# AdaLN projections past the first 2048 columns: row tiles summed by VectorE, partitions by TensorE

## The chip, the core and the metric

The kernel runs on one core of a Trainium2 chip. The metric is the device time of one execution in microseconds, taken as the median of several runs. TensorE (PE) multiplies matrices, VectorE (DVE) and ScalarE (ACT) do elementwise work, GpSimd (POOL) a few masks, and SyncE (SP) issues most of the DMA transfers.

## What is computed

The reference is a two-layer diffusion backbone on 256 latent and 256 context tokens with 1024 channels. Cut to what matters here:

```python
for i in range(DEPTH):                                    # DEPTH = 2
    mod_x = split(silu(c)     @ w_ada[i] + b_ada[i], 6)   # w_ada[i] is (1024, 6144)
    mod_c = split(silu(c_ctx) @ w_ada[i] + b_ada[i], 6)
    hx = rmsnorm(xs, norm1_g) * (1 + mod_x[1]) + mod_x[0] # the same for cs with mod_c
    mx, mc = token_mixers(hx, hc)    # w_in, four mixers, gated branch products, w_out
    xs = xs + mod_x[2] * mx
    xs = xs + mod_x[5] * swiglu(modulate(rmsnorm(xs, norm2_g), mod_x[3], mod_x[4]))
    # the context stream cs likewise with mod_c, except in the last layer
return rmsnorm(xs, final_norm_g)
```

Each `mod` is a product of one vector (one for the latent stream, one for the context) with a matrix of 1024 rows and 6144 columns: 24 MB of weights per layer for very little arithmetic.

## The kernel before

All activations lie with channels on partitions, as tiles of 128 channels by up to 512 tokens (256 latent, then 256 context). The large weights come as one stream `wst` of chunks of eight 128 x 128 blocks. `w_load` issues a chunk's load of 512 KB on SP into one of six buffers named `raw`; `w_ensure` cuts a chunk into two parts, `whi` (a copy by ScalarE) and `wlo` (two subtractions of 128 x 512 by VectorE), two chunks ahead of their use. Every block then takes three matmuls (`mm3`) into one of four banks `mm`, by way of `linear`. The mixers and small sums use four other banks `mx`.

A layer runs in three stages. In the mixers' stage, `interleave` traces the generator `lin` (products of `w_in`, later the gates and the branch products) beside the mixers' generators, by model clocks, so that TensorE and VectorE both have work. Then `out_by_stream` multiplies by `w_out` and normalizes, and SwiGLU follows: in layer 0 two groups of 11 column tiles, each tile the two products `pa` and `pg` and the function `swi`, and after each group the product with `w_ffn_out`. Layer 0 handles 512 tokens through its end, layer 1 mostly 256. A scheduler of the framework then orders each engine's instructions by modelled readiness and priority. Matmuls of the mixers and of adaLN stay behind the products traced before them (`who["now"]`).

The first 2048 columns of adaLN of layer 0 are made at the start (`ada_now`) and the last 1024 of layer 1 in its `w_out` stage. The rest are generators in the list `fill`: `ada_steps(l, c0, w)` makes 4 `w` columns. Each call of `filler` goes one step on in the first generator of the list. A step loads the columns of one row tile (128 of the 1024 rows) into one or two `raw` buffers; the next step multiplies them on TensorE, four matmuls side by side that each fill 32 rows of the bank:

```python
for j in range(4):
    PE.matmul(ps[32 * j:32 * j + 32, 0:w], cs[:, k, :], ..., start=k == 0, stop=k == KD - 1, tile_position=(0, 32 * j))
```

`cs` holds the two conditioning vectors in columns 0 and 1 of 32, the rest zero; the sum over the eight row tiles is accumulated in the bank. At the end `ada_finish` copies the bank (ScalarE), transposes blocks of 128 columns (TensorE) and adds the bias into `mods` (VectorE). `filler` is called after most products of `lin`, in `out_by_stream`, in `swi` and after the tiles of `w_ffn_out`; with these calls all generators of both layers are done by 620 us, inside the mixers' stage of layer 0.

Of the kernel before, what the change touches and what calls it, by code (L numbers as in the profile page):

```python
# [19 lines left out]
KD = D // 128  # L20
# [10 lines left out]
# on-chip room: slots, buffers of weights (raw, cut), chunks loaded and cut ahead of their use, banks for products  # L31
# [4 lines left out]
# per layer: the mixers (ssm, mla, ret) whose products are in float32 rather than in three of float32r  # L36
FP = ("m", "sr")
# per layer: the mixers that run one after the other, and those beside them (c: conv)
MIX = ("smr c", "smr c")
# per layer: lead of the products over the mixers, what a mixer's vector time counts for, gates computed ahead  # L40
# [4 lines left out]
# columns of w_in  # L45
# [7 lines left out]
# per-channel parameters, one column per tile of 128 channels  # L53
# [22 lines left out]
def n_blocks():  # L76
    """Blocks of [128, 128] of the weights of all layers, with room for the places left free to align some."""
    return L * (70 * KD + 18 + 16 + 128 + 64 + 3 * KD * KF + 32) + (L - 1) * (64 + 11 * KD)
# [13 lines left out]
class Slots:  # L92
    """Tiles of up to 2 KiB per partition, and halves of such; a tile is given back in program order."""
# [28 lines left out]
    def pair(self, n):  # L122
        """Two tiles of [128, n], float32r."""
        return self([128, n], F32R), self([128, n], F32R)
# [16 lines left out]
def trunk(ctx: ExitStack, tc: tile.TileContext, xin: bass.AP, cin: bass.AP, par: bass.AP, con: bass.AP,  # L141
# [19 lines left out]
    class PE:  # L161
        """The tensor engine; what a mixer issues stays behind the products traced before it."""
# [71 lines left out]
    def split(hi, lo, src, scale=None):  # L234
        """hi + lo = scale * src, each of float32r."""
        if scale is None:
            A.copy(hi, src)
            tt(lo, src, hi.bitcast(F32), SUB)
        else:
            A.activation(hi, src, AF.Copy, scale=scale)  # L240
            stt(lo, src, scale, hi.bitcast(F32), MUL, SUB)
# [8 lines left out]
    clk = {"pe": 0.0, "dve": 0.0, "act": 0.0}  # L250

    def mmx(o, a, b, start, stop):
        """o (+)= a^T b, of operands in float32 (one tile) or float32r (two)."""
# [6 lines left out]
    def mmp(o, c, a, b, start, stop):  # L260
        """In float32, the products of two heads side by side: b[e] with the columns 64 e .. 64 e + 64 of a, into
        these rows and the columns c of o."""
# [8 lines left out]
    def operand(f32, src, shape, scale=None):  # L271
        """An operand of scale * src; src's own slot, where it is one, is taken over."""
# [42 lines left out]
    G.memset(cs, 0.0)  # L315
    ct = cpool.tile([128, KD, 2], F32, name="ct")
# [29 lines left out]
    def w_take(blocks, align=1):  # L346
        """The next blocks of the stream: [(array, row tile, columns)]."""
# [12 lines left out]
    def linear(arr, nk, cols, X, N, k0=0, c0=0):  # L360
        """The product of the columns c0 .. c0 + N of X with a column tile of a weight, in the same columns."""
# [8 lines left out]
    def linears_by_stream(specs, X, n):  # L370
        """Up to three products of all of X, first of the first stream's columns, then of the second's."""
# [16 lines left out]
    mods = [ppool.tile([128, 48, 2], F32, tag="mod", name=f"mod{l}") for l in range(L)]  # L388

    def ada_finish(l, c0, w, ps):  # L390
        """The modulations of the columns c0 .. c0 + 4 w, of which ps has the j-th w at the rows 32 j."""
# [12 lines left out]
    def ada_load(l, c0, w):  # L404
        """4 w columns, with as many loads in flight as there are slots."""
# [18 lines left out]
    def ada_steps(l, c0, w):  # L424
        ps = mx()
        for k in range(KD):
            tl = []
            for o in range(c0, c0 + 4 * w, 1024):
                t = wpool.tile([128, 1024], F32, tag="raw", name=nm("raw"), bufs=NRAW)
                nc.sync.dma_start(t, w_ada[l, k * 128:(k + 1) * 128, o:o + 1024])  # L430
                tl.append(t)
            yield
            who["now"] += 2
            for j in range(4):
                o = j * w % 1024
                PE.matmul(ps[32 * j:32 * j + 32, 0:w], cs[:, k, :], tl[j * w // 1024][:, o:o + w],
                          start=k == 0, stop=k == KD - 1, tile_position=(0, 32 * j), skip_group_check=True)
            who["now"] -= 2
        ada_finish(l, c0, w, ps)
        yield  # L440

# [1 line left out]
    def rsqrt(v, shape):  # L443
        """1 / sqrt(v): a first guess from the exponent, a step of third order, and one of Newton's."""
        y, s, ti = sm(shape, "rs_y"), sm(shape, "rs_s"), sm(shape, "rs_i", I32)
        with tc.high_priority():
            ts(ti, v.bitcast(I32), 1, ALU.logical_shift_right)
            ts(y.bitcast(I32), ti, -1, MUL, 0x5F3759DF, ADD)
            # y (15 - 10 s + 3 s^2) / 8 with s = v y^2, here without the factor 3 / 8
# [9 lines left out]
    def tok_sums(sums, N):  # L459
        """Sums over the partitions of lists of tiles, with tokens on partitions: [128, len(sums), N / 128]."""  # L460
# [28 lines left out]
    def bcast(r, N):  # L489
        """r [128 tokens, N / 128] -> [128, N] with a token's value on every partition."""  # L490
# [5 lines left out]
    def sq_add(acc, src, N):  # L496
        """Tiles that sum to the sum of acc's and src^2."""
# [9 lines left out]
    def stats(acc):  # L507
        """1 / rms of the tokens of a stream, on all partitions, from its sums of squares."""
# [10 lines left out]
    def norm_apply(hx, src, s, rb, ab):  # L519
        """Columns of stream s of the modulated RMSNorm, (hi, lo) per tile of channels."""  # L520
# [21 lines left out]
    def interleave(lin, others, lookahead):  # L542
        """Trace generators so that neither the tensor engine nor the vector engine falls behind the other.
        Each yields the name of what it needs from another (or None) before it goes on."""
# [34 lines left out]
    fill.append(ada_steps(0, 2048, 512))  # L579
    fill.append(ada_steps(0, 4096, 512))  # L580
# [6 lines left out]
    for l in range(L):  # L587
# [12 lines left out]
        if not last:  # L600
            fill.append(ada_steps(l + 1, 0, 512))
            fill.append(ada_steps(l + 1, 2048, 512))
            fill.append(ada_steps(l + 1, 4096, 256))

        # parameters that need arithmetic
# [19 lines left out]
        def silu2(ps_, n):  # L625
            """2 silu(ps_) in a slot."""
# [6 lines left out]
        def taps(dst, src, n, w0, nt, b):  # L633
            """dst = a depthwise convolution of src with nt taps, centred, per stream of SEQ tokens; yields after each."""
# [10 lines left out]
        def lin():  # L645
# [5 lines left out]
            def zs():  # L651
                for i in range(4):
                    R["z", i] = silu2(win("z", i, N), N)
                    yield f"+z{i}"
                    filler()

            warm = [("misc", misc_cols)] + [(c, ar(OFF["xbc"] + 128 * c)) for c in (0, 1)]
            if last:
                # the context's last tokens are normalized meanwhile
# [8 lines left out]
            for g in range(2):  # L668
                for c in (2 * g, 2 * g + 1, 4 + g, 6 + g):
# [8 lines left out]
                    filler()  # L678
            for name, nt, n, gn in (("ckv", 2, T, "kvng"), ("cq", 3, N, "qng")):
                a_ = None  # L680
                for i in range(nt):
# [6 lines left out]
                    filler()  # L688
# [5 lines left out]
            for i in range(4):  # L694
# [8 lines left out]
                filler()  # L703
            for name, n in (("rk", T), ("rq", N)):
                for i in range(2):
# [5 lines left out]
                    filler()  # L711
# [8 lines left out]
            for b in range(4):  # L720
                # centred over a head's channels, so that the scan's output is too
# [57 lines left out]
        def ssm():  # L779
            yield "misc"  # L780
            misc = R["misc"]
            # dt and the cumulative logs of the decays, tokens on partitions
# [9 lines left out]
            # log(1 + e) = 2 atanh(e / (2 + e)), e in (0, 1]  # L792
# [25 lines left out]
            # with the log of dt, the exponents of the weights of a key  # L818
# [9 lines left out]
            # their rows, by way of DRAM to all partitions  # L828
# [16 lines left out]
            for g in range(2):  # L845
# [35 lines left out]
                for hh in range(4):  # L881
# [9 lines left out]
                    for s in range(ns):  # L891
                        c0 = s * SEQ
                        k0, k1 = 2 * s, 2 * s + 1
                        # w[:, 0], w[:, 1]: the stream's two blocks of keys; of the blocks on the diagonal,
                        # a has f(0), b(1), b(0), f(1): forward and backward
# [64 lines left out]
        def rope(X, perm, cname, sname):  # L960
            """Rotate the latent columns of X in place."""
# [99 lines left out]
        def mla():  # L1061
# [25 lines left out]
            def softmax(p, n):  # L1087
                """exp(p - max) / sum over each of n equal parts of p's columns."""
# [364 lines left out]
```

## Time and profile before

| | |
|---|---|
| median of 3 runs | 1731.32 us (1730.75 to 1733.25) |
| span of the profiled execution, first to last instruction | 1726.5 us |
| TensorE busy | 1684.7 us (98%) |
| VectorE busy | 1148.5 us (67%) |
| ScalarE busy | 799.6 us (46%) |
| bytes read from HBM | 253.69 MB |

The page gives the profiled execution by its span; the median of the runs is 4.8 us above it. Busy times of TensorE are of matmuls that overlap, so a busy TensorE need not be at its peak. Stages by time: start until about 43 us, mixers and branch products of layer 0 until about 690 us, `w_out` and SwiGLU of layer 0 until about 1080 us, layer 1 until the end. The chain is what ended last, followed back from the end; in a stretch where one engine holds the chain, that engine's time is the stretch's time.

### The profile page before, as it was taken

To read this page: it belongs to the slowest core of one execution; us is meant where nothing else is said; L and a number is where in the kernel's file an instruction comes from. 1 tells how busy PE (TensorE), PEld (TensorE's weight loads), DVE (VectorE), ACT (ScalarE), POOL (GpSimd) and SP (SyncE) were. 2 spreads that over 40 slices of the span, in tenths; PEclk is the share of its full clock that TensorE was granted. 3 is DMA by queue.
4 is the path that set the end of the run, shared out by engine and by line. 5 is a ranking of instruction groups with operands and counts; after the bars stand their busy time and mean duration, and the time that the engine had idled before them with its cause. 6 is when DMAs were issued, how large, how long until landed. Compare 5 with 4: busy or idle time off the path is not lost.

```text
span 1726.5 us, 26352 instructions
## 1 busy us (share of the span) xinstructions
PE 1684.7 (98%) x10146; PEld 1421.3 (82%) x10146; DVE 1148.5 (67%) x2402; ACT 799.6 (46%) x1347; POOL 54.2 (3%) x86
## 2 busy tenths in 40 slices
PE   5999999999999999999999999999999999999998
PEld 2866776677777778998888889988778899999998
DVE  3879899877236335864433446879899957866655
ACT  3565559554224223532222224547577545444444
POOL 0020100000000000000000000001110100000000
PEclk9999999999999999999999999999999999999999
DMA  9376531422554452432222225535432266645554
GB/s 367 116 279 209 196 103 51 151 72 87 173 193 170 145 172 98 160 110 98 98 98 98 98 98 183 174 105 164 133 109 96 99 226 225 216 142 183 183 184 146
DMA packets 85102, 259.16 MB, mean 150 GB/s; under 512 B 9648, under 2 KB 18784, under 8 KB 84976
## 3 DMA queue, kind: packets, MB, share of 16 engines
q1 hardware_dynamic: 73584, 244.15, 41.4%
q10 hardware_dynamic: 10624, 12.28, 2.6%
q8 instruction: 79, 1.29, 0.3%
q0 software_dynamic: 768, 1.05, 0.3%
q14 instruction: 47, 0.39, 0.1%
HBM read 253.69 MB, written 2.18 MB: 148 GB/s over the span
## 4 chain that ended last, share of the span: by engine, by line
PE 86%; DVE 5%; DMA 4%; ACT 3%; issue 1%; POOL 0%; ACTq 0%; SPq 0%; DVEq 0%; POOLq 0%
PE mm L176 75%; PE mx L176 9%; DMA u<-drow 3%; PE mx L180 2%; ACT u L152 2%; DVE u L219 1%; DVE u L215 1%; DVE wlo L219 1%; ACT whi L157 1%; DVE u L230 1%; ACT u L157 1%; DMA raw<-wst 0%; DMA u<-xin 0%; POOL u L905 0%; DMA raw<-w_ada 0%
## 5 line engine op out<-in xcount | busy, mean ns | idle before, releaser
L176 PE MATMUL mm<-u,whi 128*128 128x256 f32 (+1 forms) x5544 | 1315.4, 330 | 3.6 <-ACT u L152 2.7
L176 PEld LDWEIGHTS mm<-u,whi 128*128 128x128 f32 x5544 | 937.6, 191 | 125.8 <-issue 26.0
L176 PE MATMUL mm<-u,wlo 128*128 128x256 f32 (+1 forms) x2772 | 909.5, 329 | 0.0
L219 DVE TENSOR_TENSOR wlo<-raw,whi 128x512 fp32r<-128x512 f32 x702 | 458.8, 689 | 398.0 <-ACT whi L157 395.9
L157 ACT CAST whi<-raw 128x1024 fp32r<-128x1024 f32 x351 | 367.9, 1048 | 591.5 <-PE mm L176 383.4
L176 PEld LDWEIGHTS mm<-u,wlo 128*128 128x128 f32 x2772 | 528.7, 191 | 46.3 <-issue 1.8
L152 ACT ACTIVATE u<-u 128x256 f32<-128x256 f32 (+5 forms) x256 | 116.9, 477 | 123.1 <-DVE u L219 68.3
L219 DVE TENSOR_TENSOR u<-u,u 128x256 f32<-128x256 f32 (+5 forms) x286 | 153.4, 558 | 10.4 <-ACT u L152 5.4
L215 DVE SCALAR_TENSOR_TENSOR u<-u,convw,u 128x510 f32<-128x510 f32 (+29 forms) x240 | 133.0, 602 | 0.0
L176 PE MATMUL mx<-u,u 128*64 128x256 f32 (+6 forms) x644 | 124.2, 388 | 6.3 <-ACT whi L157 3.0
L176 PEld LDWEIGHTS mx<-u,u 128*64 128x64 f32 (+3 forms) x644 | 76.4, 163 | 46.1 <-issue 13.4
L215 DVE SCALAR_TENSOR_TENSOR u<-u,mm 128x512 f32<-128x512 f32 (+1 forms) x132 | 72.8, 551 | 49.0 <-PE mm L176 48.3
L152 ACT ACTIVATE u<-mm 128x512 f32<-128x512 f32 (+3 forms) x148 | 72.0, 486 | 63.1 <-PE mm L176 61.7
L215 DVE SCALAR_TENSOR_TENSOR u<-u,u 128x256 fp32r<-128x256 f32 (+3 forms) x99 | 55.3, 574 | 22.8 <-ACT u L152 22.8
L157 ACT COPY u<-mx 128x512 f32<-128x512 f32 (+3 forms) x69 | 35.2, 541 | 45.6 <-PE mx L176 43.8
L176 PE MATMUL mm<-whi,u 128*128 128x512 f32 x160 | 51.6, 396 | 0.5 <-ACT u L152 0.5
L215 DVE SCALAR_TENSOR_TENSOR u<-u,par,u 128x508 f32<-128x508 f32 (+5 forms) x68 | 48.2, 718 | 0.2
L903 POOL TENSOR_SCALAR_AFFINE_SELECT u<-u 128x256 f32<-128x256 f32 x24 | 15.6, 649 | 983.3 <-DVE u L230 905.1
L215 DVE SCALAR_TENSOR_TENSOR u<-mm,mod,u 128x256 f32<-128x256 f32 x64 | 30.1, 481 | 23.6 <-PE mm L176 23.6
L176 PE MATMUL mx<-raw,cs 128*32 128x512 f32 (+1 forms) x320 | 44.1, 562 | 1.7 <-DMA raw<-w_ada 1.7
L180 PE MATMUL mx<-cons,u 128*128 128x128 f32 (+1 forms) x280 | 40.7, 274 | 2.1 <-ACT u L157 1.2
L180 PEld LDWEIGHTS mx<-cons,u 128*128 128x128 f32 (+1 forms) x280 | 31.9, 141 | 12.1 <-issue 3.0
(105 smaller groups left out, 753.1 us busy)
## 6 DMA issues: line engine op xcount, KB each, us to landing
raw<-wst SPq DMA_DIRECT2D x354, 512.0 KB, 3.3
raw<-w_ada SPq DMA_DIRECT2D x72, 512.0 KB, 4.2
u<-w_ada SPq DMA_DIRECT2D x48, 256.0 KB, 5.4
u<-drow ACTq DMA_DIRECT2D x32, 256.0 KB, 5.7
u<-xin SPq DMA_DIRECT2D x16, 256.0 KB, 4.5
u<-drow ACTq DMA_DIRECT2D x16, 128.0 KB, 4.3
spill<-u SPq DMA_DIRECT2D x8, 128.0 KB, 3.2
u<-u POOLq DMA_DIRECT2D x16, 64.0 KB, 1.9
```

What stands on the lines that cost most here:

```text
L152: nc.scalar.activation(o, *a, **k)
L157: nc.scalar.copy(o, i)
L176: PE._place(nc.tensor.matmul(*a, **k))
L180: PE._place(nc.tensor.transpose(*a, **k))
L215: V.scalar_tensor_tensor(out=o, in0=i0, scalar=s, in1=i1, op0=op0, op1=op1)
L219: V.tensor_tensor(out=o, in0=i0, in1=i1, op=op)
L230: V.tensor_scalar(out=o, in0=i0, scalar1=s1, scalar2=s2, op0=op0, op1=op1)
L903: G.affine_select(out=a_[:, 0:4:3], in_=a_[:, 0:4:3], pattern=[[0, 2], [1, 128]], compare_op=ALU.is_ge, fill=-1e5, base=0, channel_multipl ...
```

## The change

`ada_steps` now takes 1024 columns and the list of streams. VectorE multiplies each row tile (two halves of 512 columns) by that row's conditioning value of a stream, a value per partition, and adds it up in `acc`, one tile of 128 x 512 per stream and half. When all eight row tiles are summed, TensorE sums over the partitions, with `pick[:, s, :]`, a 128 x 32 matrix with ones in column `s`. For columns 2048 to 5119 of layer 1, where only the latent stream is needed, one stream is computed and two row tiles are taken per step.

```diff
+    pick = cpool.tile([128, 2, 32], F32, name="pick")
+    G.memset(pick, 0.0)
+    for s in range(2):
+        G.memset(pick[:, s, s:s + 1], 1.0)
...
-    def ada_steps(l, c0, w):
+    def ada_steps(l, c0, streams):
+        w, acc, some = 256, {}, 2 // len(streams)
+        for k0 in range(0, KD, some):
+            tl = []
+            for k in range(k0, k0 + some):
+                t = wpool.tile([128, 1024], F32, tag="raw", name=nm("raw"), bufs=NRAW)
+                nc.sync.dma_start(t, w_ada[l, k * 128:(k + 1) * 128, c0:c0 + 1024])
+                tl.append((k, t))
+            yield
+            for (k, t), s, h in itertools.product(tl, streams, range(2)):
+                th, c = t[:, 512 * h:512 * h + 512], cs[:, k, s:s + 1]
+                if k == 0:
+                    acc[s, h] = U([128, 512])
+                    ts(acc[s, h], th, c, MUL)
+                else:
+                    stt(acc[s, h], th, c, acc[s, h], MUL, ADD)
+        yield
         ps = mx()
-        for k in range(KD):
...
+        who["now"] += 2
+        for i, s in enumerate(streams):
             for j in range(4):
-                o = j * w % 1024
-                PE.matmul(ps[32 * j:32 * j + 32, 0:w], cs[:, k, :], tl[j * w // 1024][:, o:o + w],
-                          start=k == 0, stop=k == KD - 1, tile_position=(0, 32 * j), skip_group_check=True)
-            who["now"] -= 2
+                PE.matmul(ps[32 * j:32 * j + 32, 0:w], pick[:, s, :], acc[s, j // 2][:, j % 2 * w:j % 2 * w + w],
+                          start=i == 0, stop=i == len(streams) - 1, tile_position=(0, 32 * j), skip_group_check=True)
+        who["now"] -= 2
+        for t in acc.values():
+            U.put(t)
         ada_finish(l, c0, w, ps)
         yield
...
-    fill.append(ada_steps(0, 2048, 512))
-    fill.append(ada_steps(0, 4096, 512))
+    for c0 in range(2048, 6144, 1024):
+        fill.append(ada_steps(0, c0, (0, 1)))
...
-            fill.append(ada_steps(l + 1, 0, 512))
-            fill.append(ada_steps(l + 1, 2048, 512))
-            fill.append(ada_steps(l + 1, 4096, 256))
+            for c0 in range(0, 5120, 1024):
+                fill.append(ada_steps(l + 1, c0, (0, 1) if c0 < 2048 else (0,)))
...
             for j in range(j, b):
                 pa = linear(fin, KD, ar(128 * j), hx, N)
+                filler()
                 pg = linear(fin, KD, ar(FFN + 128 * j), hx, N)
                 swi(pa, pg)
```

The calls of `filler` after the products of `z`, `xbc`, `ckv`, `cq`, `conv`, `rk` and `rq` in `lin` and those in `out_by_stream` are taken out. What stays are the calls in the branch products at the end of `lin` (32 in layer 0), in `swi` and after the tiles of `w_ffn_out`; a second call per column tile of SwiGLU is new.

What the order of instructions becomes, at three places. In SP's queue early in layer 0's mixers, where `wst` are chunks of weights, before:

```order
L327 DMA raw_582<-wst 128x1024
L430 DMA raw_706<-w_ada 128x1024
L430 DMA raw_708<-w_ada 128x1024
L327 DMA raw_711<-wst 128x1024
L430 DMA raw_764<-w_ada 128x1024
L430 DMA raw_766<-w_ada 128x1024
```

and now:

```order
L331 DMA raw_586<-wst 128x1024
L331 DMA raw_710<-wst 128x1024
L331 DMA raw_760<-wst 128x1024
L331 DMA raw_807<-wst 128x1024
L331 DMA raw_854<-wst 128x1024
```

Two loads of `w_ada` stood there after each chunk of weights; they now come later, one or two to a chunk, from the branch products on.

On TensorE in the branch products of layer 0 (`mm` are banks of weight products, `mx` the adaLN bank, `cons` the identity for a transpose), before:

```order
L176 MATMUL mm_4700<-u_4586,whi_4593 128x512
L176 MATMUL mm_4700<-u_4587,whi_4593 128x512
L176 MATMUL mm_4700<-u_4586,wlo_4594 128x512
L176 MATMUL mx_4366<-raw_4654,cs 32x512 x2
L176 MATMUL mx_4366<-raw_4656,cs 32x512 x2
L176 MATMUL mm_4727<-u_305,whi_4631 128x512
```

and now, where a group of 1024 columns ends:

```order
L176 MATMUL mm_4500<-u_4390,wlo_4398 128x512
L176 MATMUL mx_4515<-u_3969,pick 32x256 x2
L176 MATMUL mx_4515<-u_3971,pick 32x256 x2
L176 MATMUL mx_4515<-u_3973,pick 32x256 x2
L176 MATMUL mx_4515<-u_3975,pick 32x256 x2
L176 MATMUL mm_4534<-u_309,whi_4435 128x512
L176 MATMUL mm_4534<-u_310,whi_4435 128x512
L176 MATMUL mm_4534<-u_309,wlo_4436 128x512
L176 MATMUL mm_4534<-u_311,whi_4435 128x512
L180 MATMUL mx_4526<-cons,u_4524 128x128 x2
```

A set of four matmuls of 512 columns stood after every branch tile; now eight of 256 columns stand once per group, read from VectorE's sums, with the transposes four products behind them.

On VectorE in SwiGLU of layer 0 (a column tile is the silu step `stt` from `mm`, the product `tt` with `mm`, the cut of the result, and two chunks' `wlo`), before:

```order
L219 TENSOR_TENSOR wlo_7121<-raw_7006,whi_7120 128x512
L215 SCALAR_TENSOR_TENSOR u_7109<-u_7109,mm_7077 128x512
L219 TENSOR_TENSOR wlo_7121<-raw_7006,whi_7120 128x512
L219 TENSOR_TENSOR u_7109<-u_7109,mm_7045 128x512
L215 SCALAR_TENSOR_TENSOR u_7113<-u_7109,u_7112 128x512
L219 TENSOR_TENSOR wlo_7153<-raw_7046,whi_7152 128x512 x2
```

and now:

```order
L219 TENSOR_TENSOR u_7268<-u_7268,mm_7198 128x512
L215 SCALAR_TENSOR_TENSOR u_7190<-raw_7318,cs,u_7190 128x512
L215 SCALAR_TENSOR_TENSOR u_7192<-raw_7318,cs,u_7192 128x512
L215 SCALAR_TENSOR_TENSOR u_7272<-u_7268,u_7271 128x512
L215 SCALAR_TENSOR_TENSOR u_7194<-raw_7318,cs,u_7194 128x512
L219 TENSOR_TENSOR wlo_7324<-raw_7199,whi_7323 128x512 x2
L215 SCALAR_TENSOR_TENSOR u_7188<-raw_7364,cs,u_7188 128x512
L215 SCALAR_TENSOR_TENSOR u_7190<-raw_7364,cs,u_7190 128x512
L215 SCALAR_TENSOR_TENSOR u_7192<-raw_7364,cs,u_7192 128x512
L215 SCALAR_TENSOR_TENSOR u_7194<-raw_7364,cs,u_7194 128x512
L215 SCALAR_TENSOR_TENSOR u_7188<-raw_7402,cs,u_7188 128x512
L219 TENSOR_TENSOR wlo_7370<-raw_7237,whi_7369 128x512
```

Eight additions of a row tile (those that read `raw` and `cs`) now stand in each such column tile, before, between and behind the steps that were there.

## Rows read from the trace of the kernel before

**Rows 1.** The page: span, busy times, and tenths in 40 slices of VectorE and TensorE's clock.

```profile
span 1726.5 us, 26352 instructions
...
PE 1684.7 (98%) x10146; PEld 1421.3 (82%) x10146; DVE 1148.5 (67%) x2402; ACT 799.6 (46%) x1347; POOL 54.2 (3%) x86
...
DVE  3879899877236335864433446879899957866655
...
PEclk9999999999999999999999999999999999999999
```

**Rows 2.** The chain by line: 86 to 160, 160 to 230, 370 to 440, 440 to 560 us.

```profile
by line: PE mm L176 22.2%; DMA u<-drow 21.4%; DVE u L219 13.0%; DVE u L230 9.2%; DVE wlo L219 7.2%; PE mx L176 6.5%; DVE u L215 5.4%; DMA raw<-w_ada 4.4%; issue 4.3%; PE mx L180 3.3%; ACT u L152 2.2%; POOL u L905 1.9%; ACT whi L157 1.3%; PO
...
by line: DMA u<-drow 19.7%; DVE u L215 19.1%; DVE u L219 12.8%; issue 10.4%; DVE wlo L219 8.6%; PE mm L176 7.9%; DMA raw<-wst 7.4%; ACT u L152 2.9%; DVE u L230 2.5%; POOL u L903 1.8%; PE mx L180 1.8%; POOL u L905 1.8%; ACT whi L157 1.5%; DV
...
by line: PE mm L176 65.6%; PE mx L176 29.3%; PE mx L180 5.4%
...
by line: PE mm L176 88.6%; PE mx L176 9.4%; PE mx L180 2.0%; issue 0.1%
```

**Rows 3.** Busy us by stretch: length, PE, PEld, DVE, ACT, POOL; clock, DMA share, GB/s.

```profile
43.00:86.00 43.00, 42.68 (x265) 36.20 (x266) 35.98 (x91) 23.05 (x39) 0.00 (x0) 0.99 0.35 114
86.00:160.00 74.00, 70.45 (x357) 47.24 (x354) 61.07 (x141) 42.03 (x91) 12.05 (x18) 1.00 0.72 246
160.00:230.00 70.00, 69.75 (x365) 51.31 (x365) 60.52 (x118) 34.25 (x70) 8.01 (x14) 1.00 0.58 193
...
440.00:690.00 250.00, 249.88 (x1180) 192.88 (x1178) 109.20 (x180) 75.44 (x98) 0.00 (x0) 1.00 0.46 156
690.00:1080.00 390.00, 389.73 (x2129) 339.99 (x2128) 194.42 (x362) 129.02 (x171) 0.00 (x0) 1.00 0.34 116
```

**Rows 4.** TensorE's busy us on tiles `raw` alone: the adaLN matmuls.

```profile
43.00:86.00 43.00, 2.08 (x18) 0.99 0.35 114
86.00:230.00 144.00, 17.75 (x112) 1.00 0.65 220
230.00:690.00 460.00, 24.24 (x192) 1.00 0.38 128
```

**Rows 5.** TensorE's timeline at a set of 256 columns: start us, us, instruction.

```profile
573.43 0.39 PE L176 MATMUL mm<-u,wlo 128*128 128x512 f32 x1
...
574.11 0.39 PE L176 MATMUL mm<-u,wlo 128*128 128x512 f32 x1
574.42 0.64 PE L176 MATMUL mx<-raw,cs 128*32 128x256 f32 x8
...
575.56 0.39 PE L176 MATMUL mm<-u,wlo 128*128 128x512 f32 x1
```

**Rows 6.** VectorE's groups with a value per partition: count, busy us, mean ns.

```profile
L215 DVE SCALAR_TENSOR_TENSOR u<-u,convw,u 128x510 f32<-128x510 f32 x8 | 5.6, 745 | 0.0
...
L230 DVE TENSOR_SCALAR u<-u,convw,par 128x512 f32<-128x512 f32 x4 | 2.0, 538 | 0.0
```

**Rows 7.** VectorE's timeline in SwiGLU of layer 0; in brackets idle us before, and releaser.

```profile
807.74 0.69 DVE L219 TENSOR_TENSOR wlo<-raw,whi 128x512 fp32r<-128x512 f32 x1 [4.14 <-ACT whi L157]
...
810.92 0.69 DVE L215 SCALAR_TENSOR_TENSOR u<-u,u 128x512 fp32r<-128x512 f32 x1 [0.70 <-ACT u L152]
813.18 1.29 DVE L219 TENSOR_TENSOR wlo<-raw,whi 128x512 fp32r<-128x512 f32 x2 [1.56 <-ACT whi L157]
818.62 0.69 DVE L219 TENSOR_TENSOR wlo<-raw,whi 128x512 fp32r<-128x512 f32 x1 [4.14 <-ACT whi L157]
```

**Rows 8.** The chain in order of time, 160 to 236 us: two transfers.

```profile
177.06 10.11 DMA u<-drow
...
194.11 5.20 DMA raw<-wst
```

**Rows 9.** Layer 1: TensorE after a wait, and the stretch around it with its clock.

```profile
1235.00 1.09 PE L176 MATMUL mx<-u,u 128*64 128x256 f32 x2 [2.98 <-ACT whi L157]
...
1233.00:1240.00 7.00, 5.00 (x16) 3.59 (x17) 5.32 (x12) 4.19 (x10) 2.53 (x2) 0.76 0.23 77
```

More of the change, by code (lines that the diff above doesn't have):

```diff
@@ L422, in ada_now @@
         ada_finish(l, c0, w, ps)
-    def ada_steps(l, c0, w):
-        ps = mx()
-        for k in range(KD):
[L427 to L433, printed above, removed]
-            for j in range(4):
-                o = j * w % 1024
-                PE.matmul(ps[32 * j:32 * j + 32, 0:w], cs[:, k, :], tl[j * w // 1024][:, o:o + w],
-                          start=k == 0, stop=k == KD - 1, tile_position=(0, 32 * j), skip_group_check=True)
-            who["now"] -= 2
+    def ada_steps(l, c0, streams):
[15 more added lines that the diff above has]
+        yield
+        ps = mx()
+        who["now"] += 2
+        for i, s in enumerate(streams):
+            for j in range(4):
+                PE.matmul(ps[32 * j:32 * j + 32, 0:w], pick[:, s, :], acc[s, j // 2][:, j % 2 * w:j % 2 * w + w],
[3 more added lines that the diff above has]
+            U.put(t)
         ada_finish(l, c0, w, ps)
@@ L654, in zs @@
                     yield f"+z{i}"
-                    filler()
             warm = [("misc", misc_cols)] + [(c, ar(OFF["xbc"] + 128 * c)) for c in (0, 1)]
@@ L677, in lin @@
                     yield f"+xbc{c}"
-                    filler()
             for name, nt, n, gn in (("ckv", 2, T, "kvng"), ("cq", 3, N, "qng")):
@@ L687, in lin @@
                     R[name, i] = t
-                    filler()
                     yield None
@@ L702, in lin @@
                 yield f"+gated{i}"
-                filler()
             for name, n in (("rk", T), ("rq", N)):
@@ L710, in lin @@
                     yield f"+{name}{i}"
-                    filler()
             pos = w_take([(("w_in", l), k, ar(OFF["rv"] + 128 * m)) for k in range(KD) for m in range(4)], 8)
@@ L1260, in out_by_stream @@
                     acc_ = sq_add(acc_, residual(f, ps_, ct0, s), SEQ)
-                    filler()
                 if norm is None:
```

## The prediction

> **What bounds the kernel now.** I read the busy shares of the page first [rows 1]. TensorE is busy 98% of the 1726.5 us span and VectorE 67%, and VectorE's share by slice is 7 to 9 tenths in slices 2 to 10 (layer 0's mixers) and 3 or 4 in slices 19 to 24 (SwiGLU of layer 0). So a change that moves work from TensorE to VectorE has to be judged stretch by stretch. The chain of what ended last, cut into stretches, tells where TensorE sets the end [rows 2]: from 86 to 230 us it does so only in small part (products are 22.2%, then 7.9% of the chain; broadcasts of decay rows, VectorE and weight loads hold the rest); from 370 on its products hold over 90%. The busy times by stage say the same from the other side [rows 3]: from 86 to 160 and 160 to 230 us VectorE is busy 61.07 of 74 and 60.52 of 70 us beside a TensorE that is nearly full too; from 440 to 690 it is busy 109.20 of 250, from 690 to 1080 194.42 of 390, while TensorE has no gap.
>
> **What goes.** The 160 adaLN matmuls that run as fillers (320 records) hold TensorE for 2.08 us before 86 us, 17.75 us from 86 to 230 and 24.24 us from 230 to 690, 44.08 in all [rows 4].
> - From 230 on TensorE is the chain, so all 24.24 us come off the end. The 2.08 us lie where TensorE is busy 42.68 of 43 us [rows 3]; they come off too.
> - The 17.75 us lie where others set the end. With them 32 of the 72 loads of `w_ada` leave that stretch, of 512 KB each, on the queue that also loads the weights. Below: nothing comes back, if VectorE and the broadcasts hold the pace. A loss there isn't shown by any row, though a changed order of a few VectorE rows could bring a small one. Above: TensorE is busy 70.45 + 69.75 = 140.20 of 144 us, so without 17.75 its floor is 122.45 and the gain at most 21.6; VectorE's floor, 61.07 + 60.52 = 121.59, says about the same. What lies between is read from the chain: waits for loads into `raw` are 4.4% of 74 and 7.4% of 70 us, 8.4 us, one piece of it 5.20 us at 194.11, and one broadcast of decay rows takes 10.11 us [rows 8]. The first go with the `w_ada` loads, the second may shrink. I take half of 17.75, 8.9 us, near the 8.4 us of load waits. VectorE gets no new operation in this stretch.
>
> Together 24.24 + 2.08 + 8.9 = 35.2 us.
>
> **What comes on TensorE.** Nine groups of 1024 columns: six of two streams (four of layer 0, two of layer 1) and three of one stream, so 15 sets of four 256-wide matmuls. Such a set is in the trace: between 574.11 and 575.56 us the products take 1.45 us from one `wlo` matmul to the next with a set between them, 0.68 without (573.43 to 574.11) [rows 5]. So 0.77 us a set, 15 x 0.77 = 11.6 us, all of it where TensorE has no gap. The 18 transposes behind the sums and the additions of the bias are as many as before.
>
> **What comes on VectorE.** Per two-stream group 8 row tiles x 2 streams x 2 halves = 32 operations, per one-stream group 16: 240, of which 30 are plain multiplications and 210 multiply and add. The nearest rows have the same form: 745 ns for a step of the convolution, 538 for its first [rows 6]. 30 x 0.538 + 210 x 0.745 = 173 us. Three groups and two row tiles of a fourth lie in the branch products (from about 430 us on), 104 operations, some 74 us, against 250 - 109 = 141 us that VectorE has free from 440 to 690. The other 136 lie in SwiGLU of layer 0, against 390 - 194 = 196 us free. The tightest place is a column tile of SwiGLU in which both calls of `filler` bring a row tile. A tile takes TensorE about 10.9 us (VectorE's pattern repeats from 807.74 to 818.6: its three idle pieces, 4.14, 0.70 and 1.56 us [rows 7], leave 4.5 us of work). With 8 x 0.745 = 6.0 us more that is 10.5 of 10.9 us: it fits, with 0.4 us to spare. The cover is gone once an operation takes over 6.4 / 8 = 0.80 us. I cost the moved sums at nothing.
>
> **The new waits.** TensorE is in order, and each of the nine sums waits for VectorE's last addition of its group; behind it stand the linear products. Its transposes then wait for ScalarE's copy of the sum. The program puts one filler call between the last addition and the sum, in SwiGLU half a column tile of products, 5.4 us. From below a wait is nothing (none of the old sets in the rows around 574 us waits); from above, the longest wait that I found for TensorE on another engine, 2.98 us [rows 9]: 27 us for nine. I take 0.3 us each, 2.7 us, near the lower end because the order keeps that filler call between them. The `w_ada` loads go past no other queue, but they now share six `raw` buffers with the weights in SwiGLU, where a weight that lands late would hold VectorE's cut and then TensorE; the cut runs two chunks ahead, so I cost this at nothing.
>
> **Clock.** The granted clock is full in all 40 slices [rows 1]. In layer 1 one wait of 2.98 us lies in a stretch of 7 us with a mean granted clock of 0.76 [rows 9], part of it at 1.2 GHz and the rest at 2.4: 0.24 x 7 = 1.7 us of TensorE time lost. If the sets that leave the stretch from 86 to 230 us were what kept TensorE from waiting, it would pay this several times.
>
> The Trainium skill, page "TensorE: Matmul & The Clock Gate", section "HAM oscillation — how this bites in real kernels", speaks against thinning out TensorE's work in just this way: an engine that waits for data between its bursts of products is put back to the lower clock, and pays at every burst. By that rule, the trace agrees after the wait in layer 1; whether the stretch from 86 to 230 us would get such gaps, no run shows yet.
>
> **The sum.** 35.2 - 11.6 - 2.7 = 20.9 us. The span becomes 1726.5 - 20.9 = 1705.6. The median of the runs shown, 1731.32, is 4.8 us above the span of the profiled execution; with the same 4.8 the forecast is 1710.4 us.
>
> **The rivals.**
> - *The mixers keep their pace.* From 86 to 230 us nothing comes back. For it: VectorE's 82 to 86% there, and broadcasts on the chain. Against: the load waits on the same chain. 1710.4 + 8.9 = 1719.3 us.
> - *The mixers give all.* 21.6 instead of 8.9, and sums that never wait: 1710.4 - 12.7 - 2.7 = 1695.0 us. For it: both engines' floors. Against: a chain that passes between three engines never reaches them.
> - *The clock.* TensorE, short of work from 86 to 230 us, falls to the lower level four times at 1.7 us, and the stretch gives nothing: 1710.4 + 8.9 + 6.8 = 1726.1 us. For it: the row of layer 1. Against: TensorE's idle time in the stretch is under 4 of 144 us now, and linear products stand between the mixers' steps.
> - *VectorE becomes the bound in SwiGLU (slower).* VectorE is in order, and its two waits for ScalarE in a column tile, 0.70 and 1.56 us [rows 7], need not be filled by the moved operations, which stand where the order has put them. Then a tile needs 10.5 + 2.3 = 12.8 us against 10.9, 1.9 us too much, over 34 filler calls with additions, 17 tiles: 32 us, and 1710.4 + 32 = 1742 us. It decides from 20.9 / 17 = 1.2 us a tile on. Against: in the order the additions stand on both sides of the silu steps, and the chunks cut ahead absorb the lag of four such tiles in a row.
> - *It moves nothing.* The freed TensorE time would have to be covered by a wait everywhere; TensorE without gaps from 440 on speaks against it. It goes with the rest.
>
> **How the numbers follow.** Forecast 0.50; mixers keep their pace 0.17; mixers give all 0.10; clock 0.08; VectorE bound 0.11; rest 0.04. A measurement of this kernel tells about 0.2% (3.5 us) from no change. Faster: 0.50 + 0.17 + 0.10 and half of the clock, 0.81, which I round down to 0.80 for the order of VectorE that I can't time; same 0.08 (the other half of the clock and the rest); slower 0.12. The range reaches from the second rival to past the third, 1694 to 1733 us; what is left out is VectorE as the bound and part of the rest, some 0.15. The case of the forecast alone spans 1703 to 1718.
>
> **What would show it.** Right: from 690 to 1080 us TensorE stays without a gap and the stage is longer by the sums only; VectorE near full in column tiles with two fillers; the sums' waits under 1 us; the stretch from 440 to 690 us shorter by about 10 us (15.8 out, 6 in); the products that stand at 230 us now come about 9 to 11 us earlier. Wrong: idle time of TensorE behind VectorE in SwiGLU, a granted clock under 1 between 86 and 230 us, or the start of the branch products unmoved.

## The result

The changed kernel takes 1701.5 us (median of 5 runs) against 1730.75 us before; the ratio is 0.9827, interval 0.9811 to 0.9843. That is 29 us less, where 20.9 were forecast: inside the range, 9 us under the forecast. One of the five runs, the profiled one, took 2719.2 us at a granted clock of 0.558, so the ratio is of the other four and the profile below is of the second time that the changed kernel was run. It has a span of 1698.1 us, 28.4 under the span before.

The busy times of its page, and its granted clock by slice:

```profile
PE 1651.7 (97%) x9946; PEld 1419.6 (84%) x9946; DVE 1293.8 (76%) x2646; ACT 798.5 (47%) x1351; POOL 55.4 (3%) x89
...
PEclk9999999999999999999999999999999999999999
```

TensorE lost 33 us of busy time and VectorE gained 145, which answers to [rows 1]. The busy times of the stretches of [rows 3], in the same order of columns, for the changed kernel:

```profile
43.00:86.00 43.00, 43.00 (x259) 37.94 (x259) 37.69 (x93) 23.70 (x40) 0.00 (x0) 1.00 0.31 96
86.00:160.00 74.00, 69.90 (x341) 55.23 (x340) 64.04 (x143) 45.88 (x96) 12.32 (x17) 0.99 0.45 133
160.00:230.00 70.00, 68.62 (x339) 54.95 (x339) 68.03 (x140) 37.78 (x75) 8.81 (x15) 0.99 0.36 109
...
440.00:690.00 250.00, 248.96 (x1280) 208.71 (x1279) 177.99 (x313) 87.69 (x120) 0.00 (x0) 1.00 0.50 156
690.00:1080.00 390.00, 389.66 (x2155) 334.60 (x2154) 274.92 (x499) 127.37 (x176) 0.00 (x0) 1.00 0.56 176
```

In the first three rows the DMA share falls (0.72 to 0.45 and 0.58 to 0.36 in the second and third) while VectorE does more work per microsecond: 68.03 of 70 us from 160 to 230, where it had 60.52. In the last two rows VectorE carries the moved sums and TensorE still has no gap of note.

To see where the time went, the same instruction has to be found in both traces. The cut of a chunk of weights (`whi`, ScalarE) serves: every kernel here makes 351 of them in the same order. ScalarE's timeline at the cut of chunk 30 (counted from 0), then of 90 (end of the branch products), then of 180 (start of layer 1), each for the kernel before and for the changed one:

```profile
246.43 1.05 ACT L157 CAST whi<-raw 128x1024 fp32r<-128x1024 f32 x1 [0.73 <-PE mm L176]
...
226.83 1.05 ACT L157 CAST whi<-raw 128x1024 fp32r<-128x1024 f32 x1 [0.18 <-PE mm L176]
...
674.62 1.04 ACT L157 CAST whi<-raw 128x1024 fp32r<-128x1024 f32 x1
...
634.19 1.04 ACT L157 CAST whi<-raw 128x1024 fp32r<-128x1024 f32 x1
...
1088.09 1.05 ACT L157 CAST whi<-raw 128x1024 fp32r<-128x1024 f32 x1 [0.72 <-ACT u L152]
...
1057.96 1.05 ACT L157 CAST whi<-raw 128x1024 fp32r<-128x1024 f32 x1 [0.72 <-ACT u L152]
```

The changed kernel is 19.6 us ahead at chunk 30, 40.4 at chunk 90 and 30.1 at chunk 180; at the last chunk it is 28.0 ahead. So the first stretch gave 19.6 us, the rest of the mixers 20.8, and SwiGLU took 10.3 back. The prediction's own terms, cut at the same places, are 11.0, about 20.5 and 10.6. One term is off, and it is the first stretch. (Such times come from one profiled execution of each kernel; against the medians of the runs they are good to some 3 us.)

### The profile page after: what moved, and what is told of

Same layout as the page of the kernel before. It is cut to its first block, busy times and chain, and to the rows that moved or that the text cites. A ratio compares the mean times of both kernels' runs of the same rounds, so it can differ in the third digit from the quotient of the medians.

```text
span 2717.4 us, 26247 instructions
## 1 busy us (share of the span) xinstructions
PE 2689.1 (99%) x9946; PEld 1930.1 (71%) x9946; DVE 1314.1 (48%) x2646; ACT 807.2 (30%) x1351; POOL 49.1 (2%) x89
## 3 DMA queue, kind: packets, MB, share of 16 engines
q1 hardware_dynamic: 73584, 244.15, 26.7%
## 4 chain that ended last, share of the span: by engine, by line
PE 99%; DVE 0%; ACT 0%; DMA 0%; issue 0%; SPq 0%; DVEq 0%
PE mm L176 87%; PE mx L176 9%; PE mx L180 3%; DMA u<-xin 0%; ACT u L152 0%; PE mm L180 0%; DVE rs_s L219 0%; SPq L294 0%; DVE rs_y L215 0%; DVE rs_s L215 0%; DVE u L215 0%; ACT u L157 0%; DVE u L219 0%; ACT whi L157 0%; DVE u L228 0%
## 5 line engine op out<-in xcount | busy, mean ns | idle before, releaser
L176 PE MATMUL mm<-u,whi 128*128 128x256 f32 (+1 forms) x5544 | 2023.8, 465 | 3.4 <-ACT u L152 2.7
L176 PEld LDWEIGHTS mm<-u,whi 128*128 128x128 f32 x5544 | 1287.8, 261 | 388.6 <-issue 229.4
L176 PE MATMUL mm<-u,wlo 128*128 128x256 f32 (+1 forms) x2772 | 1284.6, 464 | 0.0
L176 PEld LDWEIGHTS mm<-u,wlo 128*128 128x128 f32 x2772 | 724.7, 262 | 187.1 <-issue 107.7
L176 PE MATMUL mx<-u,u 128*64 128x256 f32 (+6 forms) x644 | 203.0, 569 | 0.0
L215 DVE SCALAR_TENSOR_TENSOR u<-raw,cs,u 128x512 f32<-128x512 f32 x210 | 147.9, 746 | 29.1 <-DMA raw<-w_ada 29.1
L219 DVE TENSOR_TENSOR u<-u,u 128x256 f32<-128x256 f32 (+5 forms) x286 | 153.3, 558 | 16.4 <-ACT u L152 11.8
L176 PE MATMUL mm<-whi,u 128*128 128x512 f32 x160 | 79.0, 581 | 0.0
L215 DVE SCALAR_TENSOR_TENSOR u<-u,u 128x512 fp32r<-128x512 f32 (+3 forms) x99 | 55.1, 570 | 15.7 <-ACT u L152 13.9
L176 PEld LDWEIGHTS mm<-whi,u 128*128 128x128 f32 x160 | 35.2, 220 | 27.0 <-issue 16.3
L1101 DVE TENSOR_REDUCE smx<-mx 128x1 f32<-128x512 f32 (+1 forms) x40 | 27.6, 690 | 44.4 <-PE mx L176 44.1
```

What stands on the lines that cost most here:

```text
L176: PE._place(nc.tensor.matmul(*a, **k))
L215: V.scalar_tensor_tensor(out=o, in0=i0, scalar=s, in1=i1, op0=op0, op1=op1)
L219: V.tensor_tensor(out=o, in0=i0, in1=i1, op=op)
L1101: V.tensor_reduce(out=m, in_=p.rearrange("p (b t) -> p b t", b=n), axis=AX.X, op=MAX, negate=True)
```

## The experiments

Theory H is the prediction's: in the first stretch TensorE's sets matter by half, and the waits for loads are some 8 us. Theory F: TensorE paces that stretch too, so that all its sets come back, 21.6 + 2.1 = 23.7 us. Theory S: the first stretch is as forecast and the moved sums are cheaper. Differences below are from the kernel before as it was run beside each; "ahead at chunk 30" is read as above.

**The changed kernel once more**, unchanged.

> The changed kernel once more, for a profile at the full clock. Theory H (half of the first stretch, as in the prediction): stage from 690 us on longer by the sums only (15 sets at 0.77 us), branch products about 10 us shorter, the first stretch about 9 to 11 us shorter, 20.9 in all. Theory F (the first stretch is paced by TensorE, and its whole 17.75 us and more come back): the first stretch 18 to 22 us shorter. Theory S (the moved sums cost less than 14.3 us): the first stretch 9 us shorter, and the sums with their waits under 8 us. Measured so far is 1701.5 us, 29.3 less than before, so H alone is 8 us short.

1700.27 us, ratio 0.9832 (0.9817 to 0.9846). Stretch by stretch it is as told above: S falls, since SwiGLU paid its 10 us, and H is 8.6 us short in the first stretch. VectorE's new operations cost what the convolution's steps had said in [rows 6]; by groups (count, busy us, mean ns, idle before):

```profile
L215 DVE SCALAR_TENSOR_TENSOR u<-raw,cs,u 128x512 f32<-128x512 f32 x210 | 148.3, 746 | 79.0 <-DMA raw<-w_ada 78.8
...
L228 DVE TENSOR_SCALAR u<-raw,cs 128x512 f32<-128x512 f32 x30 | 13.3, 481 | 12.2 <-DMA raw<-w_ada 12.2
...
L176 PE MATMUL mx<-u,pick 128*32 128x256 f32 x120 | 9.7, 387 | 0.0
```

746 ns where 745 was taken. Not foreseen: VectorE stands 91 us in all before these operations, waiting for the row tiles to land; TensorE, idle 0.3 of 390 us from 690 on, doesn't feel it. The additions come less densely for it than the tightest tile of the prediction had them. Two column tiles of SwiGLU, before and now:

```profile
777.00:799.00 22.00, 22.00 (x99) 18.22 (x98) 9.20 (x15) 6.46 (x8) 0.00 (x0) 1.00 0.26 95
...
777.00:799.00 22.00, 22.00 (x99) 18.22 (x98) 17.18 (x28) 6.35 (x8) 0.00 (x0) 1.00 0.53 166
```

VectorE is busy 17.18 of 22 us there, where the prediction had 10.5 of 10.9 for one.

**Only the place.** TensorE accumulates as before, but `filler` is called where the change calls it.

```diff
                     yield f"+z{i}"
-                    filler()
...
                     acc_ = sq_add(acc_, residual(f, ps_, ct0, s), SEQ)
-                    filler()
...
                 pa = linear(fin, KD, ar(128 * j), hx, N)
+                filler()
                 pg = linear(fin, KD, ar(FFN + 128 * j), hx, N)
```

> The kernel before, with adaLN on TensorE as it was, but its filler calls where the change has them: all 32 + 8 sets stand in the branch products and SwiGLU of layer 0. The 19.8 us of sets from before 230 us now cost in full where TensorE has no gap. H: the first stretch gives 8.9 + 2.1, so 1730.8 - 11.0 + 19.8 = 1739.6 us. F: it gives 21.6 + 2.1, so 1730.8 - 23.7 + 19.8 = 1726.9 us. S says as H.

1736.14 us, ratio 1.0039 (1.0024 to 1.0054): the place alone costs 6 us. It is 18.8 us ahead at chunk 30, nearer F's 23.7 than H's 11.0, and then pays 26.7 for what it moved. 19.8 us of sets went along, and eight transposes, about 0.9 us (the price is read further below). The rest is mostly TensorE waiting for row tiles (its weight loads from 640 to 770 us: us in total, times, longest):

```profile
PEld mx L176 <- DMA raw<-w_ada: 4.9, 4, 2.2
```

About 1 us stays unassigned. Clearing the first stretch is worth as much here as in the changed kernel, but on TensorE the moved sets eat it all. The place alone doesn't give the gain; what VectorE's sums would give in the old places, no run shows.

**No filled adaLN products.** Neither matmuls nor loads nor transposes; the modulations are the bias.

```diff
-    fill.append(ada_steps(0, 2048, 512))
-    fill.append(ada_steps(0, 4096, 512))
+    for l_, t0_, t1_ in ((0, 16, 48), (1, 0, 40)):
+        o_ = PCOL["bada"][0]
+        V.tensor_copy(mods[l_][:, t0_:t1_, :],
+                      params[l_][:, o_ + t0_:o_ + t1_].unsqueeze(2).to_broadcast([128, t1_ - t0_, 2]))
...
-            fill.append(ada_steps(l + 1, 0, 512))
-            fill.append(ada_steps(l + 1, 2048, 512))
-            fill.append(ada_steps(l + 1, 4096, 256))
```

> The kernel before without the filled adaLN products and their loads: the modulations of these columns are the bias alone. It tells the whole price of them. H: 24.2 + 2.1 + 8.9 = 35.2 us, 1695.6 us, and the changed kernel then pays 6 us for its sums. F: 24.2 + 2.1 + 21.6 = 47.9 us, 1682.9 us, and the changed kernel pays 18.6. S: 1695.6 us.

1682.37 us, ratio 0.9727 (0.9712 to 0.9741), 47.5 us less. Ahead by 19.0 us at chunk 30 and by 44.7 at chunk 90, and nothing changes after that. The first stretch gives back nearly all of the 19.8 us that the sets hold TensorE there; F had 23.7 and H 11.0. The expectation left out the transposes, 18 blocks that go too.

**Loads alone.** The loads of `w_ada` stay in their places, unread; no matmuls, modulations as in the kernel without.

```diff
     def ada_steps(l, c0, w):
-        ps = mx()
         for k in range(KD):
...
                 nc.sync.dma_start(t, w_ada[l, k * 128:(k + 1) * 128, o:o + 1024])
             yield
-            who["now"] += 2
-            for j in range(4):
...
-        ada_finish(l, c0, w, ps)
         yield
```

> As the kernel without the filled adaLN products (modulations are the bias alone), but the loads of w_ada stay where they were, unread. It splits the first stretch into TensorE's part and the loads' part. If the loads were what the stretch waited for (8.4 us on the chain), it is about 8 us slower than the kernel without them. If TensorE paced it, within 2 us of it.

1705.39 us, ratio 0.985 (0.9816 to 0.9883), 23 us more than without them; neither the 8 us nor the at most 2 of the expectation. At chunk 30 it is 1.1 us *behind* the kernel before: without one adaLN matmul the first stretch is as long as with all. Against F, then: TensorE's sets can't be all that paces it. From there to chunk 90 it gains 25.7 us, exactly what the kernel without loads gains there, so the same loads cost nothing once the mixers' decay rows are through. The stretches from 86 and from 160 us of this kernel:

```profile
86.00:160.00 74.00, 60.53 (x290) 46.94 (x289) 53.14 (x114) 37.40 (x79) 11.19 (x16) 0.91 0.75 228
160.00:230.00 70.00, 60.69 (x298) 48.56 (x298) 59.45 (x127) 36.32 (x77) 9.91 (x16) 0.93 0.57 173
```

TensorE, with less to do, stands idle 22.8 of 144 us, and VectorE 31. The longest waits of TensorE there, and then, from 100 and 110 us, its busy time and clock:

```profile
PE mx L176 <- DVE u L219: 11.8, 1, 11.8
PE mx L180 <- DVE rs_y L215: 8.0, 1, 8.0
...
100.00:110.00 10.00, 5.35 (x23) 3.53 (x21) 5.52 (x13) 3.11 (x7) 1.93 (x4) 0.89 0.78 210
110.00:120.00 10.00, 2.81 (x10) 1.67 (x11) 5.54 (x12) 5.19 (x13) 1.35 (x1) 0.50 0.73 233
```

H and F were both wrong on the mechanism. The new theory, M: loads and sets each hold the stretch, and the longer of the two is what one sees. The next two kernels test it.

**Sets alone.** The matmuls stay, on a resident table instead of the row tiles; no filled loads, and the modulations come from the table.

```diff
-                t = wpool.tile([128, 1024], F32, tag="raw", name=nm("raw"), bufs=NRAW)
-                nc.sync.dma_start(t, w_ada[l, k * 128:(k + 1) * 128, o:o + 1024])
-                tl.append(t)
+                tl.append(cons[:, 0:1024])
```

> The kernel before with its adaLN matmuls in their places, but on a resident table of constants instead of the loaded row tiles: no filled loads of w_ada at all (the modulations are wrong values). Theory L (the loads pace the stretch up to 230 us, TensorE's sets fit beside the rest): the stretch up to the 30th chunk of weights is 17 to 19 us shorter than before, as without adaLN, and only the sets after it cost, some 25 us: 1708 us. Theory F (TensorE's sets pace it too): the stretch is 0 to 5 us shorter and the time 1723 to 1730 us. Half and half gives 9 us and 1719.

1719.89 us, ratio 0.9938 (0.992 to 0.9956). 5.8 us ahead at chunk 30, 5.9 at chunk 90 and 6.4 at the end. Taking the loads away alone gives only 5.8 of 19 us: with the sets in place TensorE is busy 73.52 of 74 and 69.73 of 70 us and is itself the bound. So TensorE does hold the stretch when the loads don't. The stretch is nearly as F had it (0 to 5 us), but the time lies below F's 1723 to 1730, near the 1719 of half and half: the medians of the runs differ by 9.2 us, the two profiles by 6.2.

**Small loads.** As with the loads alone, but 16 columns of each row tile, 8 KB for 512.

```diff
-                nc.sync.dma_start(t, w_ada[l, k * 128:(k + 1) * 128, o:o + 1024])
+                nc.sync.dma_start(t[:, 0:16], w_ada[l, k * 128:(k + 1) * 128, o:o + 16])
```

> As the kernel with unread loads and no filled adaLN matmuls, but each load takes 16 columns of its row tile (8 KB) instead of 1024 (512 KB): the same number of loads in the same places of SP's queue and of the six raw buffers, without the bytes. Theory B (bytes: the weights and the broadcasts land later beside them): as without loads, 1682 to 1685 us. Theory Q (order: the weights' loads queue behind w_ada's, which wait for a free buffer): as with the full loads, 1697 to 1707 us.

1683.88 us, ratio 0.973 (0.9712 to 0.9748), 17.8 us ahead at chunk 30. The number of loads, their places on SP's queue and the six buffers are as with the full loads, so it is the bytes. What they delay shows in the landing times on `drow` (the broadcasts of decay rows, 43 to 300 us), here of the kernel before, with the sets alone, without adaLN, and with the loads alone:

```profile
DMA to landing us min/median/max: 2.6/5.4/10.2
...
DMA to landing us min/median/max: 3.0/4.6/7.3
...
DMA to landing us min/median/max: 2.9/3.8/6.2
...
DMA to landing us min/median/max: 3.1/5.4/8.3
```

and in how long ScalarE and VectorE wait for them from 86 to 230 us (us in total, times, longest), in the same four kernels:

```profile
ACT u L152 <- DMA u<-drow: 18.8, 10, 3.3
DVE u L230 <- DMA u<-drow: 12.7, 7, 4.5
...
ACT u L152 <- DMA u<-drow: 14.7, 9, 2.9
DVE u L230 <- DMA u<-drow: 2.5, 3, 1.0
...
ACT u L152 <- DMA u<-drow: 8.3, 6, 2.4
DVE u L230 <- DMA u<-drow: 1.2, 1, 1.2
...
ACT u L152 <- DMA u<-drow: 16.8, 9, 5.5
DVE u L230 <- DMA u<-drow: 10.7, 4, 3.6
```

With the loads both wait longer, with the sets and without. (With the small loads the median landing is 4.3 us.) That these waits are what lengthens the stretch fits the rows; no run delayed the broadcasts alone.

With this the first stretch is a table of four. Start of the cut of chunk 30, us:

| | without sets | with sets |
|---|---|---|
| without loads | 227.4 | 240.6 |
| with loads | 247.5 | 246.4 |

Taken out of the kernel before, the sets are worth -1.1 us, the loads 5.8, both 19.0. A step down a column is the loads alone: up to chunk 30 the two kernels of a column have the same order of instructions on TensorE, VectorE and ScalarE. A step along a row is the sets and the order with them: all kernels without sets there, the changed one too, share on TensorE and ScalarE one order, which is not that of the kernel before. No run parts the two. What the order can have done is read from TensorE's busy time from 43 us to the cut of chunk 30, in the kernel before, the changed one, the one without adaLN, with the sets alone and with the loads alone (length, PE, PEld, DVE, ACT, POOL; clock, DMA share, GB/s):

```profile
43.00:246.43 203.43, 199.30 (x1061) 148.12 (x1061) 173.68 (x382) 105.93 (x209) 20.07 (x32) 1.00 0.56 189
...
43.00:226.83 183.83, 178.35 (x922) 145.66 (x922) 166.59 (x369) 104.28 (x206) 21.14 (x32) 0.99 0.39 117
...
43.00:227.41 184.41, 178.72 (x924) 145.82 (x924) 166.08 (x370) 103.77 (x205) 20.28 (x32) 0.99 0.38 116
...
43.00:240.58 197.58, 196.82 (x1067) 148.70 (x1066) 174.98 (x385) 106.94 (x210) 18.31 (x32) 1.00 0.36 112
...
43.00:247.50 204.50, 181.72 (x928) 147.93 (x928) 167.63 (x372) 105.04 (x207) 21.10 (x32) 0.94 0.61 188
```

In the first four TensorE is idle 4.1, 5.5, 5.7 and 0.8 us: its own work nearly fills the stretch, in either order, and the changed kernel, 19.6 us shorter, has 21 us less of that work. Only with the loads alone is it idle for 22.8 us. Its busy time there is 3.0 us longer than without the loads, at a granted clock of 0.94 against 0.99, so of the 20 us that the loads cost without the sets some 3 can be the clock, and 17 are waits. So M holds as far as this: TensorE's work is the one bound, the delayed mixers the other. How long the mixers with the loads would take in the order of the kernel before, without its sets, stays open.

**More work on VectorE.** The changed kernel with 120 more multiplications of 128 x 512 whose result nothing reads.

```diff
                     stt(acc[s, h], th, c, acc[s, h], MUL, ADD)
+                if h == 0:
+                    d_ = acc.setdefault("d", None) or U([128, 512])
+                    acc["d"] = d_
+                    ts(d_, th, c, MUL)
```

> The changed kernel with one more multiplication of a half row tile per row tile and stream, whose result nothing reads: 120 more operations of 0.48 us on VectorE, 4 in a column tile of SwiGLU with two fillers, where it then needs 4.5 + 6.0 + 1.9 = 12.4 us in TensorE's 10.9. Theory V (VectorE without room, as the slower rival had it): 17 such tiles at 1.5 us, 1726 us. Theory C (the chunks cut ahead and the light steps between groups absorb it): 1700 to 1704 us.

1704.32 us, ratio 0.9848 (0.9826 to 0.987): 4 us more than the changed kernel (5 by the profiled spans) for some 58 us of work (120 x 0.48). Theory C holds, at its upper end. The stage from 690 to 1080 us:

```profile
690.00:1080.00 390.00, 388.02 (x2134) 332.40 (x2133) 299.91 (x561) 126.61 (x175) 0.00 (x0) 1.00 0.55 175
```

TensorE's idle time there is 2 us instead of 0.3: the cover begins to give, and is far from gone.

**The sums twice.** Each sum of the changed kernel is done a second time; the second begins the bank anew, so the modulations are the same (the expectation says they double; they don't).

```diff
-        for i, s in enumerate(streams):
+        for i, s in [*enumerate(streams), *enumerate(streams)]:
```

> The changed kernel with every sum over the partitions done twice into the same bank (the modulations are twice the sums): 15 sets of 256 columns more on TensorE, and no wait that wasn't there. If a set costs 0.77 us as the prediction had it, 11.6 us more than the changed kernel, 1712 us. If the sums are mostly covered by waits that TensorE has anyway, under 5 us more, 1705.

1709.18 us, ratio 0.9882 (0.9865 to 0.99): 8.9 us more than the changed kernel, 0.59 us for each of 15 sets. The sums lie in the open, as forecast, at three quarters of the price. TensorE's timeline at one two-stream sum of the changed kernel:

```profile
473.62 0.39 PE L176 MATMUL mm<-u,wlo 128*128 128x512 f32 x1
...
474.30 0.39 PE L176 MATMUL mm<-u,wlo 128*128 128x512 f32 x1
474.62 1.07 PE L176 MATMUL mx<-u,pick 128*32 128x256 f32 x16
...
476.20 0.40 PE L176 MATMUL mm<-u,wlo 128*128 128x512 f32 x1
```

From `wlo` to `wlo` it is 1.90 us with two sets between and 0.68 without: 1.22 us for the pair, 0.61 a set. The row of [rows 5] was of a set alone. So are the three sums of one stream, here with the two transposes behind one of them:

```profile
919.98 0.39 PE L176 MATMUL mm<-u,wlo 128*128 128x512 f32 x1
920.30 0.64 PE L176 MATMUL mx<-u,pick 128*32 128x256 f32 x8
...
921.44 0.39 PE L176 MATMUL mm<-u,wlo 128*128 128x512 f32 x1
...
922.13 0.39 PE L176 MATMUL mm<-u,wlo 128*128 128x512 f32 x1
922.36 0.38 PE L180 MATMUL mx<-cons,u 128*128 128x128 f32 x2
...
923.05 0.40 PE L176 MATMUL mm<-u,wlo 128*128 128x512 f32 x1
```

The lone set costs 1.46 - 0.68 = 0.78 us, the pair of transposes 0.92 - 0.69 = 0.23. Why a set is cheaper beside another, these rows don't show. Six pairs and three lone sets make 9.7 us.

## Why the prediction was right, and where it was short

- **What goes from 230 us on: right.** 24.24 us were forecast; the kernel without adaLN gains 25.7 us between chunks 30 and 90, transposes included.
- **What goes before: the step that failed is "I take half of 17.75, 8.9 us, near the 8.4 us of load waits".** With the 2.08 us that made 11.0; the changed kernel was 19.6 us ahead at chunk 30. The upper bound, 21.6 us for the stretch from 86 to 230 alone, was nearly reached. I had read the chain's shares as the price of each cause, so much for the sets and so much for the loads, and halved. The table of four shows that they don't share the stretch: each alone holds most of it, so each alone is worth little, and the change takes out both. That TensorE's own work could be the price stood in the busy times: it is idle only 4.1 of 203.4 us up to chunk 30. That the changed kernel comes near that floor, idle 5.5 us, is because the loads went too; with the sets gone alone it was idle 22.8. The reason against "the mixers give all", that a chain which passes between three engines never reaches the floors, didn't hold here. The chain also booked only the waits for `raw` as the loads' doing. Waits for broadcasts, `DMA u<-drow`, hang on the loads too: they land at 3.8 us in the median without the loads and at 5.4 with them (at 4.6 and 5.4 where the sets stay). The prediction said that they may shrink and gave that no price. And of the 32 loads that it counted out of the stretch from 86 to 230 us, 25 are issued in it and 7 before it, from 56 us on.
- **What comes on TensorE: right in kind, a little high.** 11.6 us forecast, 8.9 by doubling and 9.7 by the timeline: the lone set was read rightly, but twelve of the fifteen stand in pairs. The waits at the sums, 2.7 us forecast, came out lower. The changed kernel lost 10.3 us from chunk 90 to 180: four pairs of sets are 4.9, three lone ones 2.3, seven pairs of transposes, which stood before chunk 90 in the kernel before, 1.6, and 1.3 are waits for VectorE, all at the sum at 638.82 us (TensorE's weight loads for the sums in this stretch; us in total, times, longest):

```profile
PEld mx L176 <- DVE u L215: 1.3, 3, 0.5
```

- **What comes on VectorE: right.** 746 and 481 ns against 745 and 538; beyond TensorE's matmuls the sums cost 1.3 us of waits. VectorE near full in column tiles with two fillers, a sign that the prediction named, wasn't seen in the two from 777 us: 17.18 of 22 us. The slower rival put 1.9 us too much into each of 17 column tiles; with a further 58 us on VectorE the kernel grew by only 4.
- **The clock: right to leave it out.** In the changed kernel the granted clock is 0.99 and 0.99 in the two stretches, 0.91 and 0.92 in the 10 us before and behind 160, where TensorE waits 2.4 us; before it was 1.00. That is the sign of being wrong that the prediction named, at a size that decides nothing: 0.09 + 0.08 of 10 us. It did fall where TensorE really waited, to 0.50 (the level of 1.2 GHz) from 110 to 120 us with the loads alone, in and behind the wait of 11.8 us, which ended at 117 us. The rule of the Trainium skill, page "TensorE: Matmul & The Clock Gate", section "HAM oscillation — how this bites in real kernels", that waiting for data puts the engine back to the lower clock, agrees with that row. It didn't decide here: with sets and loads both gone, TensorE's longest wait in the stretch is those 2.4 us.
- **Layer 1.** The lead fell from 30.1 to 28.0 us there, without any changed instruction of adaLN. The kernel with small loads loses 2.4 us at the same place (chunks 200 to 220) and the one without adaLN nothing; the layer's code is the same in all. I put it down to no part of the change.

In sum 11.0 became 19.6 and the other terms held to within 3 us each; 20.9 us became 28.4 in the profiled spans.

## What to carry to other kernels

When two causes hold a stretch at once, their shares of the chain are not their prices: take each out alone and both together before halving anything, since a change that removes both may get the whole stretch. Ask of every moved load what else is landing at that time; the cost of its bytes can show as longer waits for other transfers, under their names. And work taken out of a stage has to land on an engine that idles in its new place: here the place alone, still on TensorE, lost 6 us, and together with the engine it gained 29. The engine alone was not run.

## What the runs showed of the hardware

- With 32 loads of 512 KB over some 136 us beside them, broadcasts of 128 and 256 KB on another queue landed at 5.4 us in the median instead of 3.8, and the stage was 20 us longer, some 3 of it perhaps by the clock; the same number of loads of 8 KB cost 1.2 us. The same large loads cost nothing later: from chunk 30 to 90 both kernels gain 25.7 us.
- Two sets of four 128 x 32 matmuls of 256 columns in float32, back to back, cost 1.22 us together; one alone among other matmuls cost 0.77 and 0.78.
- A float32 multiply and add of VectorE with a value per partition takes 746 ns for 128 x 512, and the plain multiplication 481.
